# Last stage of a hybrid attention block on whole rows of 1024 columns, with the embedding vectors loaded earlier

## The chip, the cores and the metric

The kernel runs on one core of a Trainium2 chip. The metric is device time in microseconds (us), taken as the median of several runs. Before the change it is 712.65 us, the median of 3 runs (712.34 to 713.63). A separate execution was recorded by the hardware profiler; the lines shown in this document come from that one.

## The reference: what is computed

The reference is one decoder block over 528 positions (16 meta tokens and 512 inputs) of width 1024. After an input LayerNorm, ten projections are taken, two attention branches are computed and gated, the branches are merged and projected, and a residual LayerNorm gives the output. What matters for this change is the input LayerNorm, which is recomputed for the residual, and the end:

```python
h = layer_norm(h, emb_ln_g, emb_ln_b)
...
br_d = jnp.einsum('blw,wd->bld', y_d * jax.nn.silu(g_d), w_br_diff[i])
br_s = jnp.einsum('blw,wd->bld', y_s * jax.nn.silu(g_s), w_br_sb[i])
merged = jax.nn.sigmoid(m_d + b_gate[i, 0]) * br_d + jax.nn.sigmoid(m_s + b_gate[i, 1]) * br_s
y = jnp.einsum('bld,de->ble', merged, w_out[i])
h = layer_norm(DN_ALPHA * h + y, ln_g[i], ln_b[i])
...
return h[:, N_META:].astype(x.dtype)
```

## The kernel before

**Numbers and splitting.** Every product of float32 matrices is done as three matrix products of a high and a low part (`hh`, `hl`, `lh`). A weight arrives by DMA as a half tile `raw` (128 x 4 x 128), ScalarE (ACT) casts it to its high part `wh` (`hi`, line 183), and VectorE (DVE) subtracts to get the low part `wl` (`lo`, line 188). Both come from rings of six buffers, one ring for `wh` and one for `wl`; they are made four halves ahead of their use (`prep`, `state["ahead"]`).

**Stages.** First comes the input LayerNorm with its transposes. Then there are sixteen attention units (eight differential heads, eight pairs of stick-breaking heads), in which TensorE (PE) does the projections of the next unit (lines 494 to 496, 510, 690) between the scores (754), transposes (766) and values of this one. `stage_q` (line 604) makes a unit's queries; its second half, line 612, is a DVE operation `low` that reads a PSUM bank. Then come the merge gates of the first branch, four pairs of branch products ("BD", line 1065), the second set of merge gates (line 1099), four pairs "BS", and the last stage.

**What sets the order.** Each engine executes its own queue in order. For the attention units the order inside each queue is found by the framework's scheduler, which works from a model of time and from when the buffers come free; only the order in which work is written is given. From the merge gates on (`first`, line 1026) `keep_order` (line 1229) fixes the written order on PE, DVE, ACT, POOL (GpSimd) and SP, whose queue issues most DMAs.

**The last stage** (lines 1145 to 1229) makes y for 4 blocks `t` of 128 positions times 2 halves `c` of 512 columns. The loop runs over `c` outside and `t` inside. For each (c, t), 24 products of line 1190 fill one of three PSUM banks `pso`; the very last one, c=1 and t=3, is made as two banks of 256 columns. DVE then adds the residual (1198) and takes statistics (1201). With c=1 the row is complete: 1206 aggregates, POOL computes the reciprocal root `frs` (lines 296 and 297), and `shift` (1211) and `scale` (1215) apply the LayerNorm, in the order shift of half 0, scale of half 0, shift of half 1, scale of half 1. For t=3 a quarter row is scaled on ACT (1221) and POOL (1222) instead. Line 1227 stores two halves per block.

The residual `hr` is a half row of x, 128 x 512, loaded by line 1157 into a buffer of the `wh` or `wl` ring; lines 1161 and 1162 apply the input LayerNorm to it with the vectors `eg` and `eb`, of which line 1154 loads a half, spread over all partitions. `load_half(0)` and `load_half(1)` issue two such vectors and four half rows each. Between the blocks, `MEANWHILE` (line 1175) places on DVE the residuals and the splitting of the second half of `w_out` (`split_out`, lines 1126 and 1127, whose `fetch` issues the next load of `w_out` on SP). The vectors of the output LayerNorm, `lgb`, are loaded from ACT's queue (1196, 1197).

Of the kernel before, what the change touches and what calls it, by code (L numbers as in the profile page):

```python
# [45 lines left out]
def hybrid_block_kernel(ctx: ExitStack, tc: tile.TileContext, x, meta, emb_g, emb_b, w_in, b_gate,  # L46
# [128 lines left out]
    def hi(h):  # L175

        assert len(split) == h
        item = items[h]
# [4 lines left out]
        s.copy(wh, raw)  # L183
# [961 lines left out]
    def half(tag, name):  # L1145
        return wpool.tile([P, 4, P], F32, tag=tag, name=name, bufs=6).rearrange("p a b -> p (a b)")

    vec, hrs = {}, [[None, None] for t in range(NB)]

    def load_half(c):  # L1150
        tag = ("wh", "wl")[c]
        for name, src in (("eg", emb_g), ("eb", emb_b)):
            vec[name, c] = half({"eg": "wh", "eb": "wl"}[name], name)
            nc.sync.dma_start(vec[name, c], src[ts(c, 512)].partition_broadcast(P))
        for t in range(NB):
            hrs[t][c] = half(tag, "hr")
            nc.sync.dma_start(hrs[t][c], x[0, ts(t, P), ts(c, 512)])

    def residual(t, c):
        hr = hrs[t][c]  # L1160
        v.scalar_tensor_tensor(hr, hr, xmv[:, t, 0:1], vec["eg", c], op0=ALU.subtract, op1=ALU.mult)
        v.scalar_tensor_tensor(hr, hr, xrs[:, t:t + 1], vec["eb", c], op0=ALU.mult, op1=ALU.add)
# [12 lines left out]
    MEANWHILE = [[lambda: residual(0, 0)] + [lambda k=k: split_out(1, k) for k in range(3)],
                 [lambda: residual(1, 0)] + [lambda k=k: split_out(1, k) for k in range(3, 6)],
                 [lambda: residual(2, 0)] + [lambda k=k: split_out(1, k) for k in range(6, 8)] + [lambda: residual(0, 1)],
                 [lambda: residual(3, 0)] + [lambda t=t: residual(t, 1) for t in range(1, 3)],
                 [lambda: residual(3, 1)], [], [], []]
    for c in range(2):  # L1180
        for t in range(NB):
            st, final = sts[t], t == NB - 1
            for o, w in [(0, 256), (256, 256)] if final and c else [(0, 512)]:
                r, hr = ds(o, w), hrs[t][c]
# [24 lines left out]
            def shift(c, o, w):  # L1209
                a = hrs[t][c][:, ds(o, w)]  # L1210
                v.scalar_tensor_tensor(a, a, mv[:, 0:1], lgb[0][:, ds(512 * c + o, w)], op0=ALU.subtract, op1=ALU.mult)

            def scale(c, o, w):
                a = hrs[t][c][:, ds(o, w)]
                v.scalar_tensor_tensor(a, a, rs, lgb[1][:, ds(512 * c + o, w)], op0=ALU.mult, op1=ALU.add)  # L1215
# [43 lines left out]
```

## Time and profile before

| what | value |
|---|---|
| runs of the kernel before, us | 713.63, 712.65, 712.34 |
| the profiled execution, us | 712.22 |
| its span in the trace, us | 710.4 |
| PE busy, share of the span | 98% |
| DVE busy | 80% |
| ACT busy | 62% |
| POOL busy | 18% |

The profiled execution took 712.22 us, of which the trace's span covers 710.4. A row of a timeline has the start in us from the start of the span, the busy time in us, the engine, the source line, the operation, the tiles written and read, shapes, how often it came in a row, and in brackets the idle time before it with what ended it. "SPq" and "ACTq" are the queues of engines that issue DMAs. PE's operations are pipelined, so that a matmul of 512 columns shows 0.39 us, while the next one starts 0.23 us after it.

### The profile page before, as it was taken

To read this page: it belongs to the slowest core of one execution; us is meant where nothing else is said; L and a number is where in the kernel's file an instruction comes from. 1 tells how busy PE (TensorE), PEld (TensorE's weight loads), DVE (VectorE), ACT (ScalarE), POOL (GpSimd) and SP (SyncE) were. 2 spreads that over 40 slices of the span, in tenths; PEclk is the share of its full clock that TensorE was granted. 3 is DMA by queue.
4 is the path that set the end of the run, shared out by engine and by line. 5 is a ranking of instruction groups with operands and counts; after the bars stand their busy time and mean duration, and the time that the engine had idled before them with its cause. 6 is when DMAs were issued, how large, how long until landed. Compare 5 with 4: busy or idle time off the path is not lost.

```text
span 710.4 us, 13389 instructions
## 1 busy us (share of the span) xinstructions
PE 697.5 (98%) x4494; PEld 636.9 (90%) x4494; DVE 571.8 (80%) x1265; ACT 439.2 (62%) x1065; POOL 125.6 (18%) x143
## 2 busy tenths in 40 slices
PE   9999999999999999999999999999999999999994
PEld 8999999989999898988989998988889998999884
DVE  6888897878787777988878889976666788788897
ACT  5766676757667587776857777666455546455300
POOL 3214210212222111212123120000012102220002
PEclk9999999999999999999999999999999999999997
DMA  9368754879888876899897976646576748795902
GB/s 293 93 169 164 167 133 125 184 181 183 198 200 184 201 177 164 186 215 214 200 217 174 206 171 175 166 133 197 178 174 112 164 123 182 133 198 170 322 15 104
DMA packets 182182, 123.36 MB, mean 174 GB/s; under 512 B 9009, under 2 KB 165074, under 8 KB 182114
## 3 DMA queue, kind: packets, MB, share of 16 engines
q1 hardware_dynamic: 148130, 102.32, 50.1%
q0 software_dynamic: 33664, 19.14, 21.6%
q10 hardware_dynamic: 320, 1.06, 0.4%
q8 instruction: 35, 0.57, 0.3%
q14 instruction: 33, 0.27, 0.1%
HBM read 91.96 MB, written 9.44 MB: 143 GB/s over the span
## 4 chain that ended last, share of the span: by engine, by line
PE 86%; DVE 6%; DMA 3%; ACT 2%; issue 1%; POOL 1%; SPq 0%; ACTq 0%; DVEq 0%; POOLq 0%
PE q L690 16%; PE ps L496 12%; PE ps L494 12%; PE ps L495 12%; PE q L1065 10%; PE ps L510 7%; PE sc L754 6%; PE t L766 4%; DMA lgb<-in_ln_b_dram 1%; PE bank L385 1%; PE tv L723 1%; DVE hr L1215 1%; DMA xt<-in_x_dram 1%; PE av L922 1%; DMA raw<-in_w_out_dram 1%
## 5 line engine op out<-in xcount | busy, mean ns | idle before, releaser
L188 DVE TENSOR_TENSOR wl<-raw,wh 128x512 fp32r<-128x512 f32 x169 | 115.7, 691 | 43.7 <-ACT wh L183 42.2
L494 PE MATMUL ps<-hTh,wh 128*128 128x512 f32 x368 | 145.0, 394 | 0.0
L495 PE MATMUL ps<-hTl,wh 128*128 128x512 f32 x368 | 144.5, 393 | 0.0
L496 PE MATMUL ps<-hTh,wl 128*128 128x512 f32 x368 | 144.4, 392 | 0.0
L183 ACT CAST wh<-raw 128x512 fp32r<-128x512 f32 x169 | 104.4, 625 | 28.0 <-PE ps L495 15.3
L496 PEld LDWEIGHTS ps<-hTh,wl 128*128 128x128 f32 x368 | 69.2, 188 | 13.9
L495 PEld LDWEIGHTS ps<-hTl,wh 128*128 128x128 f32 x368 | 69.2, 188 | 13.1
L494 PEld LDWEIGHTS ps<-hTh,wh 128*128 128x128 f32 x368 | 69.2, 188 | 12.9
L146 POOL DMA_DIRECT2D rawk<-in_w_in_dram x44 | 60.8, 1642 | 96.9 <-DMA rawk<-in_w_in_dram 58.4
L754 PE MATMUL sc<-k,A 128*128 128x264 f32 (+3 forms) x320 | 65.9, 299 | 0.1
L1065 PE MATMUL q<-gh,wh 128*128 128x256 f32 x224 | 63.5, 283 | 0.2 <-ACT t L1074 0.2
L1065 PE MATMUL q<-gl,wh 128*128 128x256 f32 x224 | 63.4, 283 | 0.0
L1065 PE MATMUL q<-gh,wl 128*128 128x256 f32 x224 | 63.4, 283 | 0.0
L907 DVE TENSOR_TENSOR_SCAN e<-e,diag 128x528 f32<-128x528 f32 (+1 forms) x64 | 53.4, 848 | 7.5 <-ACT e L901 7.3
L754 PEld LDWEIGHTS sc<-k,A 128*128 128x128 f32 x320 | 50.3, 189 | 3.3 <-ACT e L901 0.3
L690 PE MATMUL q<-tS,wh 128*128 128x264 f32 x176 | 50.9, 290 | 0.9 <-DVE low L612 0.9
L690 PE MATMUL q<-tl,wh 128*128 128x264 f32 x176 | 50.2, 286 | 0.0
L690 PE MATMUL q<-tS,wl 128*128 128x264 f32 x176 | 50.2, 286 | 0.0
L510 PE MATMUL ps<-hTh,wh 128*128 128x264 f32 x160 | 46.4, 290 | 0.2 <-ACT k L632 0.2
L933 POOL DMA_DIRECT2D ys<-half x14 | 11.8, 840 | 195.9 <-ACT ys L932 119.2
L510 PE MATMUL ps<-hTh,wl 128*128 128x264 f32 x160 | 45.6, 286 | 0.0
L510 PE MATMUL ps<-hTl,wh 128*128 128x264 f32 x160 | 45.5, 285 | 0.0
(291 smaller groups left out, 1851.4 us busy)
## 6 DMA issues: line engine op xcount, KB each, us to landing
raw<-in_w_in_dram SPq DMA_DIRECT2D x141, 256.0 KB, 3.3
rawk<-in_w_in_dram POOLq DMA_DIRECT2D x44, 256.0 KB, 6.0
rawk<-in_w_in_dram SPq DMA_DIRECT2D x33, 256.0 KB, 3.9
k<-ks SPq DMA_DIRECT2D x60, 132.0 KB, 3.1
raw<-in_w_out_dram SPq DMA_DIRECT2D x16, 256.0 KB, 3.9
k<-ks SPq DMA_DIRECT2D x60, 66.0 KB, 2.8
A<-low SPq DMA_DIRECT2D x28, 128.0 KB, 2.8
raw<-in_w_br_diff_dram SPq DMA_DIRECT2D x12, 256.0 KB, 4.7
```

What stands on the lines that cost most here:

```text
L146: second[l] = [lambda raw=raw, x=x: g.dma_start(raw, x, accum_op=ALU.add) for x in more]
L183: s.copy(wh, raw)
L188: eng.tensor_tensor(wl, raw, wh.bitcast(F32), op=ALU.subtract)
L494: pe.matmul(ps, wh[:, k % 4, :], hTh[:, k, M:], start=(k == 0), stop=False)
L495: pe.matmul(ps, wh[:, k % 4, :], hTl[:, k, M:], start=False, stop=False)
L496: pe.matmul(ps, wl[:, k % 4, :], hTh[:, k, M:], start=False, stop=(k == KT - 1))
L510: pe.matmul(ps[:, :H2], a[:, k % 4, :], b[:, k, ts(c, H2)], start=(k == 0 and m == 0), stop=(k == KT - 1 and m == 2))
L690: pe.matmul(bank, a[:, k, :], b, start=start and k == 0 and j == 0, stop=k == 3 and j == 2, skip_group_check=not start)
L754: pe.matmul(ps[:, :n], q, K[:, m, k0:k0 + n], start=(m == 0), stop=(m == 1))
L766: pe.transpose(t[:, o:o + P], a[:, AOFF[i] + j * P:AOFF[i] + (j + 1) * P], ident)
L907: v.tensor_tensor_scan(rev, rev, diag[0][:, L - nk:][:, ::-1], 0.0, ALU.mult, ALU.max)
L1065: pe.matmul(bank, a[:, k, :], b[:, n, k, :], start=start and k == 0 and m == 0, stop=k == 3 and m == 2, skip_group_check=not start)
```

## The change

There are four edits.

- `wh` and `wl` of a weight half become two halves of one tile `w2` in one ring of six buffers.
- `eg` and `eb` are loaded whole, 1024 columns each, from SP, between the pairs "BD" and the second set of merge gates, into the ring "two" of `pair_of`.
- The last stage works on whole rows. A row of x is one load of 128 x 1024 into a buffer of `w2`; `residual(t)` is two DVE operations of 1024 columns. Row 0 is loaded after `split_out(0, 5)`, rows 1 to 3 behind the residual of the row before. `lgb` takes two buffers of `w2` and is loaded when t=2. In `MEANWHILE` the splitting stands ahead of the residual.
- `shift` is one operation of 1024 columns, and `scale` follows it directly, also 1024 columns wide; for t=3 it is two of 512 columns, each followed by its store. The quarter on ACT and POOL is gone. Blocks 0 to 2 are stored by one DMA each.

```diff
-        wh, wl = [wpool.tile([P, 4, P], F32R, tag=w, name=w, bufs=6) for w in ("wh", "wl")]
+        w2 = wpool.tile([P, 2, 4, P], F32R, tag="w2", name="w2", bufs=6)
+        wh, wl = w2[:, 0], w2[:, 1]
...
     ss = [pair_of("ss", n=S) for j in range(3)]
+    vec = {}
+    for name, src in (("eg", emb_g), ("eb", emb_b)):
+        vec[name] = pair_of(name, n=512).rearrange("p a b -> p (a b)")
+        nc.sync.dma_start(vec[name], src.partition_broadcast(P))
...
+    def load_rows(t):
+        hrs.append(whole("hr"))
+        nc.sync.dma_start(hrs[t], x[0, ts(t, P), :])
+
+    def residual(t):
+        hr = hrs[t]
+        v.scalar_tensor_tensor(hr, hr, xmv[:, t, 0:1], vec["eg"], op0=ALU.subtract, op1=ALU.mult)
+        v.scalar_tensor_tensor(hr, hr, xrs[:, t:t + 1], vec["eb"], op0=ALU.mult, op1=ALU.add)
...
-    load_half(0)
     for k in range(5, KT):
         split_out(0, k)
-    load_half(1)
+        if k == 5:
+            load_rows(0)
...
-    MEANWHILE = [[lambda: residual(0, 0)] + [lambda k=k: split_out(1, k) for k in range(3)],
...
+    MEANWHILE = [[lambda k=k: split_out(1, k) for k in range(3)] + [lambda: residual(0), lambda: load_rows(1)],
...
-                    if t == 0 and c == 0:
-                        nc.scalar.dma_start(lgb[0][:, :], ln_g[0].partition_broadcast(P))
-                        nc.scalar.dma_start(lgb[1][:, :], ln_b[0].partition_broadcast(P))
+                    if t == 2 and c == 0:
+                        for src in (ln_g, ln_b):
+                            lgb.append(whole("lgb"))
+                            nc.scalar.dma_start(lgb[-1], src[0].partition_broadcast(P))
...
-            shift(0, 0, 512)
-            if final:
-                a = hrs[t][1][:, 256:]
-                shift(1, 256, 256)
-                s.mul(a, a, rs)
-                g.tensor_tensor(a, a, lgb[1][:, 768:], op=ALU.add)
-            scale(0, 0, 512)
-            shift(1, 0, 256 if final else 512)
-            scale(1, 0, 256 if final else 512)
-            for h in range(2):
-                nc.sync.dma_start(out[0, ts(t, P), ts(h, 512)], hrs[t][h])
+            shift(0, D)
+            if not final:
+                scale(0, D)
+                nc.sync.dma_start(out[0, ts(t, P), :], hrs[t])
+                continue
+            scale(0, 512)
+            nc.sync.dma_start(out[0, ts(t, P), :512], hrs[t][:, :512])
+            scale(512, 512)
+            nc.sync.dma_start(out[0, ts(t, P), 512:], hrs[t][:, 512:])
```

The instructions move in three places. The first is DVE's queue at the end of the program, from the statistics of block t=3 on. Before:

```order
L1198 SCALAR_TENSOR_TENSOR hr<-hr,pso 128x256
L1201 BN_STATS fst<-hr 128x6
L1206 BN_AGGR fmv<-fst 128x2
L1211 SCALAR_TENSOR_TENSOR hr<-hr,fmv,lgb 128x512
L1211 SCALAR_TENSOR_TENSOR hr<-hr,fmv,lgb 128x256
L1215 SCALAR_TENSOR_TENSOR hr<-hr,frs,lgb 128x512
L1211 SCALAR_TENSOR_TENSOR hr<-hr,fmv,lgb 128x256
L1215 SCALAR_TENSOR_TENSOR hr<-hr,frs,lgb 128x256
```

The same place after the change, where the line numbers are one less:

```order
L1197 SCALAR_TENSOR_TENSOR hr<-hr,pso 128x256
L1200 BN_STATS fst<-hr 128x6
L1205 BN_AGGR fmv<-fst 128x2
L1210 SCALAR_TENSOR_TENSOR hr<-hr,fmv,lgb 128x1024
L1214 SCALAR_TENSOR_TENSOR hr<-hr,frs,lgb 128x512 x2
```

Five operations behind the aggregate have become three, and the shift of the whole row stands ahead of the first scaling, which needs POOL's `frs`.

The second place is SP's queue from the last loads of `w_out` to the stores. Before:

```order
L144 DMA raw<-in_w_out_dram 128x512 x11
L1154 DMA eg<-in_emb_ln_g_dram 128x512
L1154 DMA eb<-in_emb_ln_b_dram 128x512
L1157 DMA hr<-in_x_dram 128x512 x4
L144 DMA raw<-in_w_out_dram 128x512 x3
```

Behind these five rows stand a second group of `eg`, `eb` and four half rows, the last two loads of `w_out`, and eight stores. After the change there is in their place:

```order
L144 DMA raw<-in_w_out_dram 128x512 x12
L1157 DMA hr<-in_x_dram 128x1024
L144 DMA raw<-in_w_out_dram 128x512 x4
L1157 DMA hr<-in_x_dram 128x1024 x3
L1219 DMA out_dram<-hr 128x1024 x3
```

All sixteen loads of `w_out` now stand ahead of the rows 1 to 3, with row 0 between them.

The third place lies in an attention unit of the stick-breaking branch. There the scheduler has drawn up all queues anew, since the buffers of `wh` and `wl` now come free together. DVE's queue around the last `low` of `stage_q` (`e` and `apad` belong to the scores of a unit, `al` and `ax` to its transposes, `sg` to a gate), before:

```order
L188 TENSOR_TENSOR wl<-raw,wh 128x512
L907 SCALAR_TENSOR_TENSOR e_447<-e_447,diag 128x528
L772 TENSOR_TENSOR al_6114<-t_6108,ah_6113 128x512
L908 TENSOR_TENSOR apad_433<-e_446,e_447 128x527
L788 TENSOR_TENSOR ax<-t_6120,own_block 128x128
L612 SCALAR_TENSOR_TENSOR low<-ps,A_6137 128x512
L524 TENSOR_TENSOR sg<-ps,sg 128x512
L188 TENSOR_TENSOR wl<-rawk,wh 128x512
```

And after the change, where a low part is called `w_` with a number:

```order
L189 TENSOR_TENSOR w_6113<-raw,w_6113 128x512
L908 SCALAR_TENSOR_TENSOR e_443<-e_443,diag 128x528
L909 TENSOR_TENSOR apad_429<-e_442,e_443 128x527
L189 TENSOR_TENSOR w_6148<-rawk,w_6148 128x512
L773 TENSOR_TENSOR al_5970<-t_5964,ah_5969 128x512
L789 TENSOR_TENSOR ax<-t_5976,own_block 128x128
L613 SCALAR_TENSOR_TENSOR low<-ps,A_5993 128x512
L525 TENSOR_TENSOR sg<-ps,sg 128x512
```

Here the low part made from `rawk` has moved from behind the gate to ahead of `low`. Such moves run through all units of the attention stage on PE, DVE, ACT and SP; POOL's queue keeps its order, but for the operation of line 1222, which is gone.

More of the change, by code (lines that the diff above doesn't have):

```diff
@@ L1142, in hybrid_block_kernel, with whole @@
         run([pair("BS", p, G, MS[2 * p:2 * p + 2], lambda m, p=p: merged(2 * p + m))], steps)
[L1145 to L1162, printed above, removed]
+    def whole(name):
+        return wpool.tile([P, 2, 4, P], F32, tag="w2", name=name, bufs=6).rearrange("p a b c -> p (a b c)")
+    hrs = []
+    def load_rows(t):
[5 more added lines that the diff above has]
+        v.scalar_tensor_tensor(hr, hr, xrs[:, t:t + 1], vec["eb"], op0=ALU.mult, op1=ALU.add)
     for _, f in later:
@@ L1166, in hybrid_block_kernel @@
     later.clear()
-    load_half(0)
     for k in range(5, KT):
         split_out(0, k)
-    load_half(1)
+        if k == 5:
+            load_rows(0)
     WO.append([lp.tile([P, KT, 512], F32R, tag=f"g{x}", name=f"wo1{x}") for x in "hl"])
-    lgb = [pair_of("lgb", n=512) for j in range(2)]
-    lgb = [t.rearrange("p a b -> p (a b)") for t in lgb]
+    lgb = []
     sts = [lr.tile([P, 4, 6], F32, tag="fst", name="fst", bufs=4) for t in range(NB)]
-    MEANWHILE = [[lambda: residual(0, 0)] + [lambda k=k: split_out(1, k) for k in range(3)],
[L1176 to L1179, printed above, removed]
+    MEANWHILE = [[lambda k=k: split_out(1, k) for k in range(3)] + [lambda: residual(0), lambda: load_rows(1)],
+                 [lambda k=k: split_out(1, k) for k in range(3, 6)] + [lambda: residual(1), lambda: load_rows(2)],
+                 [lambda k=k: split_out(1, k) for k in range(6, 8)] + [lambda: residual(2), lambda: load_rows(3)],
+                 [lambda: residual(3)], [], [], [], []]
     for c in range(2):
@@ L1183, in hybrid_block_kernel @@
             for o, w in [(0, 256), (256, 256)] if final and c else [(0, 512)]:
[L1184 removed]
+                r, hr = ds(o, w), hrs[t][:, ts(c, 512)]
                 ps = pj.tile([P, 512], F32, tag="pj", name="pso")[:, :w]
@@ L1207, in hybrid_block_kernel, with shift, scale @@
             rstd_of(lr, mv[:, 1:2], rs, P)
[L1209 to L1215, printed above, removed]
-            shift(0, 0, 512)
-            if final:
-                a = hrs[t][1][:, 256:]
-                shift(1, 256, 256)
-                s.mul(a, a, rs)
-                g.tensor_tensor(a, a, lgb[1][:, 768:], op=ALU.add)
-            scale(0, 0, 512)
-            shift(1, 0, 256 if final else 512)
-            scale(1, 0, 256 if final else 512)
-            for h in range(2):
-                nc.sync.dma_start(out[0, ts(t, P), ts(h, 512)], hrs[t][h])
+            def shift(o, w, t=t, mv=mv):
+                a = hrs[t][:, ds(o, w)]
+                v.scalar_tensor_tensor(a, a, mv[:, 0:1], lgb[0][:, ds(o, w)], op0=ALU.subtract, op1=ALU.mult)
+            def scale(o, w, t=t, rs=rs):
+                a = hrs[t][:, ds(o, w)]
+                v.scalar_tensor_tensor(a, a, rs, lgb[1][:, ds(o, w)], op0=ALU.mult, op1=ALU.add)
+            shift(0, D)
[7 more added lines that the diff above has]
+            nc.sync.dma_start(out[0, ts(t, P), 512:], hrs[t][:, 512:])
     keep_order(state["ends"], ORDERED[:1])
```

## The prediction

> **What bounds the kernel now.** The page and the time by stretches come first, since they say where there is room at all.
>
> ```profile
> span 710.4 us, 13389 instructions
> 30.00:560.00 530.00, 528.70 (x3415) 482.71 (x3414) 424.99 (x983) 359.66 (x901) 98.71 (x98) 1.00 0.77 178
> 701.00:711.00 10.00, 0.00 (x0) 0.00 (x0) 6.06 (x12) 0.51 (x1) 1.78 (x3) 0.59 0.27 106
> ```
>
> The first pair of columns is PE with its instructions, the third DVE. From 30 to 560 us PE is busy for 528.70 of 530 us at full granted clock (1.00): all room there is 1.3 us. From 701 us on PE does nothing, and DVE works for 6 us. So the end must be read from the timeline of the last stage: PE's first and last row there, then the other engines.
>
> ```profile
> 656.42 0.40 PE L1190 MATMUL pso<-wo0h,mh 128*128 128x512 f32 x1
> 700.40 0.28 PE L1190 MATMUL pso<-wo1h,ml 128*128 128x256 f32 x1
> 701.95 0.41 DVE L1198 SCALAR_TENSOR_TENSOR hr<-hr,pso 128x256 f32<-128x256 f32 x1
> 702.40 0.43 DVE L1201 BATCH_NORM_STATS2 fst<-hr 128x6 f32<-128x256 f32 x1
> 702.74 0.40 DVE L1198 SCALAR_TENSOR_TENSOR hr<-hr,pso 128x256 f32<-128x256 f32 x1
> 703.18 0.43 DVE L1201 BATCH_NORM_STATS2 fst<-hr 128x6 f32<-128x256 f32 x1
> 703.64 0.26 DVE L1206 BATCH_NORM_AGGREGATE fmv<-fst 128x2 f32<-128x24 f32 x1
> 703.94 1.17 DVE L1211 SCALAR_TENSOR_TENSOR hr<-hr,fmv,lgb 128x512 f32<-128x512 f32 x2
> 705.16 0.75 DVE L1215 SCALAR_TENSOR_TENSOR hr<-hr,frs,lgb 128x512 f32<-128x512 f32 x1
> 705.83 0.97 DVE L1211 SCALAR_TENSOR_TENSOR hr<-hr,fmv,lgb 128x256 f32<-128x256 f32 x1
> 706.83 0.48 DVE L1215 SCALAR_TENSOR_TENSOR hr<-hr,frs,lgb 128x256 f32<-128x256 f32 x1
> 704.25 0.87 POOL L297 TENSOR_TENSOR frs<-lne,neghalf 128x1 f32<-128x1 f32 x1
> 690.56 17.15 SPq L1227 DMA_DIRECT2D out_dram<-hr  x8
> ```
>
> PE's last product ends at 700.40 + 0.28 = 700.7, but DVE takes up the second-to-last bank only at 701.95 and the last at 702.74: it is 2.0 us behind PE. Its last operation ends at 706.83 + 0.48 = 707.3; the last store is issued at once (690.56 + 17.15 = 707.7 ends the issue), and the span ends at 710.4, 3.1 us behind DVE. So DVE sets the end. The block before, with the same half c=1, shows why it is behind:
>
> ```profile
> 696.93 0.68 DVE L1198 SCALAR_TENSOR_TENSOR hr<-hr,pso 128x512 f32<-128x512 f32 x1
> 697.64 0.69 DVE L1201 BATCH_NORM_STATS2 fst<-hr 128x6 f32<-128x512 f32 x1
> 698.37 0.21 DVE L1206 BATCH_NORM_AGGREGATE fmv<-fst 128x2 f32<-128x12 f32 x1
> 698.62 0.78 DVE L1211 SCALAR_TENSOR_TENSOR hr<-hr,fmv,lgb 128x512 f32<-128x512 f32 x1
> 699.84 0.75 DVE L1215 SCALAR_TENSOR_TENSOR hr<-hr,frs,lgb 128x512 f32<-128x512 f32 x1 [0.44 <-POOL frs L297]
> 700.50 0.74 DVE L1211 SCALAR_TENSOR_TENSOR hr<-hr,fmv,lgb 128x512 f32<-128x512 f32 x1
> 701.28 0.75 DVE L1215 SCALAR_TENSOR_TENSOR hr<-hr,frs,lgb 128x512 f32<-128x512 f32 x1
> ```
>
> A block costs DVE 701.95 - 696.93 = 5.02 us, of which 0.44 is a wait for POOL. PE needs (700.7 - 656.4) / 8 = 5.5 us per block of 512 columns, so DVE gains only half a microsecond per block and carries its lag from the first half of the stage to the end.
>
> **The change part by part: shift and scale.** The width of 1024 stands in the trace once, on DVE, in another stage:
>
> ```profile
> 587.03 1.23 DVE L1047 TENSOR_TENSOR gl<-t,gh 128x1024 fp32r<-128x1024 f32 x1 [0.18 <-ACT gh L1046]
> ```
>
> From 256 to 512 columns L1215 goes from 0.48 to 0.75 us, 0.27 per 256 columns; two such steps more are 1.29 us for 1024. The row of 1.23 is a simpler operation and agrees. The bounds are 1.23 and twice 0.75 = 1.50; I take 1.29. An operation that does not depend on the one ahead starts 0.66 us after it at 512 columns (699.84 to 700.50), one that does 0.78 (700.50 to 701.28), so 0.09 before or 0.04 behind its end. [...]
>
> Blocks 0 to 2 of c=1 then cost 1.44 (696.93 to 698.37) + 0.25 + 1.33 + 1.21 = 4.23 us instead of 5.02. The wait for POOL is covered: `frs` ended 705.12 - 703.90 = 1.22 us behind the aggregate's end in the last block, and the shift of 1024 columns takes 1.29 of that. If the cover were gone, it would cost the 0.44 again.
>
> The last block: from the aggregate's start to the end of the last scaling stand 707.31 - 703.64 = 3.67 us before. After: 0.30 + 1.33 (shift) + 0.66 + 0.75 (two scalings) = 3.04. That is 0.63 less, and POOL and ACT, beside which a shift of 256 columns took 0.97 us, have left.
>
> **The lag.** If DVE waits for PE at the end, the last bank is taken up at about 700.8, not 702.74, and the tail starts at 700.8 + (703.64 - 702.74) = 701.7: 1.94 us earlier. PE's own time stays (same 24 products per bank). So the question is whether DVE catches up, which the first half of the stage decides:
>
> ```profile
> 659.43 1.89 DVE L1127 TENSOR_TENSOR wo0l<-raw,wo0h 128x512 fp32r<-128x512 f32 x3
> 663.03 0.75 DVE L1161 SCALAR_TENSOR_TENSOR hr<-hr,xmv,eg 128x512 f32<-128x512 f32 x1 [1.71 <-DMA hr<-in_x_dram]
> 660.15 3.19 SPq L144 DMA_DIRECT2D raw<-in_w_out_dram  x3
> hr<-in_x_dram SPq DMA_DIRECT2D x8, 256.0 KB, 5.9
> 658.86 10.32 DMA lgb<-in_ln_b_dram
> ```
>
> Row 0 is issued behind the load that SP issued at 660.15, so at about 660.6. With the median of 5.9 us it lands at 666.5. Ahead of it DVE splits three parts (659.43 to 661.3) and three more (1.9 us), until 663.2: the old wait of 1.7 us becomes one of about 3.3. From then on, with a residual at 1.33 + 1.21 = 2.54, a split at 1.89 / 3 = 0.63 and L1198 with L1201 at 1.4, the four blocks of c=0 (three splits in the second, two in the third) cost 3.94, 5.83, 5.20 and 3.94, in all 18.9, so DVE is at 685.4 when PE's fifth bank is ready (656.4 + 5 x 5.5 = 684). Three blocks of 4.23 end at 698.1. Bound by PE, the third block would start when its bank is ready, at 700.7 - 5.5 = 695.2, and end at 699.4; the two quarters need 0.79 ahead of the last bank. So DVE has about 0.5 us in hand at the end, and another 1.3 at the start: row 0 may land as late as 668.3. The Trainium skill ("DMA: Bandwidth & Descriptors", section "Anatomy of one DMA") puts a transfer at 2.0 us plus its bytes by 436 GB/s, by which the whole row lands 0.6 us later than a half and speaks against joining loads; by it the row lands at 663.8 (an estimate: 3.2 us), by the rows at 666.5, and the sum is the same by both.
>
> **Loads.** The vectors stand on SP ahead of the loads for the first pair "BS":
>
> ```profile
> 584.35 0.37 SPq L144 DMA_DIRECT2D raw<-in_w_br_sb_dram  x1
> 589.77 2.59 POOL L146 DMA_DIRECT2D rawa<-in_w_br_sb_dram  x2 [30.86 <-DMA rawa<-in_w_br_sb_dram]
> rawa<-in_w_br_sb_dram POOLq DMA_DIRECT2D x8, 256.0 KB, 5.9
> 604.03 0.62 ACT L183 CAST wh<-rawa 128x512 fp32r<-128x512 f32 x1
> out_dram<-hr SPq DMA_DIRECT2D x8, 256.0 KB, 2.0
> ```
>
> Two issues of about 0.4 us and 1 MB are added. Their buffers held `ydT`, whose last readers ran before the pairs "BD", so SP waits for nothing. Behind them queue the `raw` and `rawa` loads, for these POOL's adding DMAs, for those ACT's cast at 604.03. That chain ends at 589.77 + 2.59 + 5.9 = 598.3, 5.8 us ahead of the cast. A vector of this size took 10.32 us in the crowded last stage (the `lgb` row above), 4.4 more than a half row there; a delay of 4.4 is within the 5.8, so I take nothing. Without that cover a late cast would hold up PE by what exceeds it. The last two loads of `w_out` lose their place behind eight half rows, and DVE's waits for them go. The stores of block 3 come 0.7 us apart instead of 1.4; each takes 2.0 us, which bounds the cost by 1.3 us; the DMA engines are 0.27 busy there (701 to 711 us, above), so I take nothing.
>
> **The attention stage.** The queues are drawn up anew, as the third place above shows. What ACT's cast waited for, and PE from 30 us on (us in all, times, longest):
>
> ```profile
> L183 ACT CAST wh<-raw 128x512 fp32r<-128x512 f32 x169 | 104.4, 625 | 28.0 <-PE ps L495 15.3
> PE q L690 <- DVE low L612: 0.9, 2, 0.6
> PE ps L510 <- ACT k L632: 0.2, 1, 0.2
> PE q L1065 <- ACT t L1074: 0.2, 1, 0.2
> 440.15 0.39 PE L690 MATMUL q<-tS,wh 128*128 128x264 f32 x1 [0.63 <-DVE low L612]
> ```
>
> The ring `w2` makes the cast wait for the product behind L495, 5.5 / 24 = 0.23 us later; PE uses the tile four halves later, so I take nothing. For the new order the bound below is all idle time, 1.3 us of gain. Above, a wait like the one at 440.15 in each of 15 units would be 15 x 0.63 = 9.5 us. I take zero: the same scheduler with the same work, and in the old order two waits in all; it is nearest to that row.
>
> **Sum.** 1.94 + 0.63 = 2.57 us less, span 707.9. Against the profiled execution's 712.2 that is 709.6; this execution lay 0.4 under the median of 712.65, so for the median 710.1 us. About 0.2%, 1.4 us, can be told from no change.
>
> **The rivals.** (1) The new order costs PE 1.2 to 4 us in the attention stage, so that the gain is eaten: 711.3 to 714.1. For it speaks that a low part now stands ahead of the last `low`, 0.6 us on DVE, just where PE waited; against it that the other operations ahead of it are the same as before. Chance 0.2. (2) DVE does not catch up, since row 0 comes late: from 668.3 on each microsecond is lost. With the 10.3 us that `lgb` took, it lands at 670.9, the loss is 2.6, and the time 712.7. Against it: `lgb` shared its time with ten other transfers, row 0 with five. Chance 0.07. (3) Slower: PE waits at L690 for `low` once per unit. From 4.0 us more of such waits (2.6 + 1.4) the kernel is slower than before; that is eight units at 0.63 less the 0.9 there now, 714.2, and with all 15 it is 718.7. Against it: in the old order two units did. Chance 0.08. (4) The new order removes PE's waits: 0.9 to 1.3 more, 709. Chance 0.08.
>
> **How the numbers follow.** The forecast has 0.57: 709.2 to 711.2, from the 0.2 to 0.3 by which the wide operations may differ five times and the stores. Faster by over 0.2% (under 711.2) are the forecast, (4), and 0.04 of the edges of (1) and (2): 0.69. Within 0.2%: the rest of (1) but its upper end, and of (2): 0.21. Slower: (3) and 0.02 of (1): 0.10. The range reaches from 708.9, rival (4), to 712.7, which leaves out (3) and the upper part of (1).
>
> **What would show it.** Right: in the last block DVE's L1198 waits for PE in both quarters, no wait for `frs`, operations of 1.29 us, DVE's end near 704.7, PE's last product still near 700.4. Wrong: PE's last product later than 701.5 (the attention stage has paid), or DVE without waits for PE in blocks 1 to 3 of c=1, or a wait for `hr` of more than 5 us.

## The result, and the profile after

| | before | after |
|---|---|---|
| runs, median (lowest to highest), us | 712.36 (711.76 to 713.63), 10 runs | 710.65 (710.26 to 711.77), 10 runs |
| profiled execution, us | 712.22 | 710.71 |
| span, us | 710.4 | 708.9 |
| PE's first and last product of the last stage start at, us | 656.42, 700.40 | 657.05, 701.04 |
| DVE takes up the last bank at, us | 702.74 | 701.36 |
| aggregate of the last block starts at, us | 703.64 | 702.27 |
| last scaling ends at, us | 707.31 | 705.74 |

The ratio is 0.9979 (95% interval 0.997 to 0.9988): 1.7 us faster where 2.57 were forecast. The first rows of the timeline after show DVE in the first half of the last stage, with SP's issue of row 0:

```profile
657.05 0.40 PE L1188 MATMUL pso<-wo0h,mh 128*128 128x512 f32 x1
661.15 0.42 SPq L1157 DMA_DIRECT2D hr<-in_x_dram  x1
661.86 1.89 DVE L1132 TENSOR_TENSOR wo1l<-raw,wo1h 128x512 fp32r<-128x512 f32 x3
665.12 1.29 DVE L1161 SCALAR_TENSOR_TENSOR hr<-hr,xmv,eg 128x1024 f32<-128x1024 f32 x1 [1.37 <-DMA hr<-in_x_dram]
684.73 0.69 DVE L1197 SCALAR_TENSOR_TENSOR hr<-hr,pso 128x512 f32<-128x512 f32 x1 [0.29 <-PE pso L1188]
```

DVE waits 1.37 us for row 0, although it has already done three splits that stood behind that wait before. At 684.73 it is the other way round: DVE waits for PE's fifth bank. It has caught up before the half c=1 begins. The same timeline from the block t=2 of c=1 to the end:

```profile
695.61 0.69 DVE L1197 SCALAR_TENSOR_TENSOR hr<-hr,pso 128x512 f32<-128x512 f32 x1 [0.71 <-PE pso L1188]
697.30 1.31 DVE L1210 SCALAR_TENSOR_TENSOR hr<-hr,fmv,lgb 128x1024 f32<-128x1024 f32 x1
699.05 1.29 DVE L1214 SCALAR_TENSOR_TENSOR hr<-hr,frs,lgb 128x1024 f32<-128x1024 f32 x1 [0.44 <-POOL frs L298]
700.25 0.41 DVE L1197 SCALAR_TENSOR_TENSOR hr<-hr,pso 128x256 f32<-128x256 f32 x1
701.04 0.28 PE L1188 MATMUL pso<-wo1h,ml 128*128 128x256 f32 x1
701.36 0.42 DVE L1197 SCALAR_TENSOR_TENSOR hr<-hr,pso 128x256 f32<-128x256 f32 x1 [0.23 <-PE pso L1188]
702.27 0.26 DVE L1205 BATCH_NORM_AGGREGATE fmv<-fst 128x2 f32<-128x24 f32 x1
702.57 1.31 DVE L1210 SCALAR_TENSOR_TENSOR hr<-hr,fmv,lgb 128x1024 f32<-128x1024 f32 x1
704.32 1.42 DVE L1214 SCALAR_TENSOR_TENSOR hr<-hr,frs,lgb 128x512 f32<-128x512 f32 x2 [0.44 <-POOL frs L298]
```

Three things are to be seen. DVE takes up the last bank 0.32 us behind PE, still waits for `frs`, and PE itself is late. In numbers, the last bank is taken up 701.36 - 701.04 = 0.32 us after the start of PE's last product, where it was 702.74 - 700.40 = 2.34: the lag is 2.02 us shorter. The wait for `frs` is still there, 0.44 us, in spite of a shift of 1.31 us beside which POOL works; so the tail from the aggregate's start to the last scaling's end is 705.74 - 702.27 = 3.47 us, 0.20 less than the 3.67 before. And PE's own last product is 0.64 us later. With 0.07 more between DVE's end and the span's end, that makes -2.02 - 0.20 + 0.64 + 0.07 = -1.51 us, which is the difference of the two spans.

Two things needed an experiment: why the wait for POOL stayed, and what made DVE catch up and PE late. The profile alone cannot tell which of the four edits did which.

### The profile page after: what moved, and what is told of

Read it like the earlier page. It is cut to its first block, busy times and chain, and to the rows that moved or that the text cites. A ratio compares the mean times of both kernels' runs of the same rounds, so it can differ in the third digit from the quotient of the medians.

```text
span 708.9 us, 13322 instructions
## 1 busy us (share of the span) xinstructions
PE 697.0 (98%) x4494; PEld 636.0 (90%) x4494; DVE 569.3 (80%) x1249; ACT 438.3 (62%) x1064; POOL 126.8 (18%) x142
## 3 DMA queue, kind: packets, MB, share of 16 engines
q10 hardware_dynamic: 320, 1.06, 0.4%
## 4 chain that ended last, share of the span: by engine, by line
PE 90%; ACT 3%; issue 2%; DMA 2%; DVE 2%; POOL 1%; POOLq 0%; DVEq 0%; SPq 0%; ACTq 0%
PE q L691 15%; PE ps L497 11%; PE ps L496 11%; PE ps L495 11%; PE q L1066 11%; PE ps L511 7%; PE pso L1188 6%; PE sc L755 5%; PE t L767 3%; PE bank L386 1%; PE tv L724 1%; DMA k<-ks 1%; PE av L923 1%; PE av L924 1%; DMA xt<-in_x_dram 1%
## 5 line engine op out<-in xcount | busy, mean ns | idle before, releaser
L189 DVE TENSOR_TENSOR w<-raw,w 128x512 fp32r<-128x512 f32 x169 | 114.8, 686 | 41.4 <-ACT w L184 39.0
L495 PE MATMUL ps<-hTh,w 128*128 128x512 f32 x368 | 145.0, 394 | 0.0
L497 PE MATMUL ps<-hTh,w 128*128 128x512 f32 x368 | 144.6, 393 | 0.0
L496 PE MATMUL ps<-hTl,w 128*128 128x512 f32 x368 | 144.3, 392 | 0.0
L184 ACT CAST w<-raw 128x512 fp32r<-128x512 f32 x169 | 104.1, 626 | 19.2 <-PE ps L497 9.9
L497 PEld LDWEIGHTS ps<-hTh,w 128*128 128x128 f32 x368 | 69.2, 188 | 13.9
L1066 PE MATMUL q<-gh,w 128*128 128x256 f32 x448 | 81.4, 283 | 0.2 <-ACT t L1075 0.2
L496 PEld LDWEIGHTS ps<-hTl,w 128*128 128x128 f32 x368 | 69.2, 188 | 13.0
L495 PEld LDWEIGHTS ps<-hTh,w 128*128 128x128 f32 x368 | 69.2, 188 | 12.8
L691 PE MATMUL q<-tS,w 128*128 128x264 f32 x352 | 75.1, 290 | 0.0
L1066 PEld LDWEIGHTS q<-gh,w 128*128 128x128 f32 x448 | 70.1, 192 | 0.5 <-ACT t L1075 0.4
L755 PE MATMUL sc<-k,A 128*128 128x264 f32 (+3 forms) x320 | 66.8, 298 | 1.3 <-DMA k<-ks 0.9
L511 PE MATMUL ps<-hTh,w 128*128 128x264 f32 x320 | 64.4, 288 | 0.2 <-ACT k L633 0.2
L755 PEld LDWEIGHTS sc<-k,A 128*128 128x128 f32 x320 | 50.3, 188 | 4.5 <-ACT e L904 1.9
L511 PEld LDWEIGHTS ps<-hTh,w 128*128 128x128 f32 x320 | 51.4, 188 | 0.6 <-ACT k L633 0.4
```

The costliest lines, as they stand in the source:

```text
L189: eng.tensor_tensor(wl, raw, wh.bitcast(F32), op=ALU.subtract)
L495: pe.matmul(ps, wh[:, k % 4, :], hTh[:, k, M:], start=(k == 0), stop=False)
L496: pe.matmul(ps, wh[:, k % 4, :], hTl[:, k, M:], start=False, stop=False)
L497: pe.matmul(ps, wl[:, k % 4, :], hTh[:, k, M:], start=False, stop=(k == KT - 1))
L511: pe.matmul(ps[:, :H2], a[:, k % 4, :], b[:, k, ts(c, H2)], start=(k == 0 and m == 0), stop=(k == KT - 1 and m == 2))
L691: pe.matmul(bank, a[:, k, :], b, start=start and k == 0 and j == 0, stop=k == 3 and j == 2, skip_group_check=not start)
```

## Experiments

All times are medians in us, compared with runs of the kernel before on the same chip (its median lay between 712.23 and 712.44). A microsecond is 0.14%.

| kernel | us (lowest to highest, runs) | ratio to before, 95% interval |
|---|---|---|
| half_blocks | 710.79 (710.27 to 712.25, 8) | 0.9978, 0.9968 to 0.9988 |
| early_vec | 710.46 (709.91 to 711.70, 9) | 0.9973, 0.9958 to 0.9987 |
| vec_late | 712.16 (711.81 to 713.08, 12) | 1.0000, 0.9991 to 1.0008 |
| ring_only | 712.75 (711.84 to 713.11, 11) | 1.0000, 0.9992 to 1.0009 |
| split_shift | 710.72 (709.41 to 711.55, 11) | 0.9975, 0.9966 to 0.9984 |
| psum_shift | 710.24 (709.68 to 711.06, 6) | 0.9969, 0.9958 to 0.9980 |
| old_rings | 709.50 (709.10 to 709.70, 5) | 0.9958, 0.9944 to 0.9971 |
| old_rings_2, old_rings_3 | 710.17 (7 runs), 709.35 (5 runs) | 0.9968, 0.9955 to 0.9980; 0.9961, 0.9947 to 0.9974 |
| after_2, after_3 | 710.26 (5 runs), 710.72 (11 runs) | 0.9970, 0.9958 to 0.9982; 0.9979, 0.9970 to 0.9988 |
| before_2 | 712.40 (1 run) | |

**Are the wide blocks what lets DVE catch up?** The changed kernel, with blocks 0 to 2 as they were:

```diff
-            shift(0, D)
-            if not final:
-                scale(0, D)
+            if final:
+                shift(0, D)
+            else:
+                for o in (0, 512):
+                    shift(o, 512)
+                    scale(o, 512)
```

> The changed kernel with the blocks 0 to 2 of c=1 as in the kernel before (shift, scale, shift, scale of 512 columns); the last block as in the changed kernel. A block then costs DVE about 5.0 us instead of 4.6 with its waits for PE (0.29, 0.44 and 0.71 us in the changed kernel, 1.44 in all), against 5.44 us that PE takes for one. Theory, that the whole-row operations of these three blocks only shorten DVE's waits for PE: 0 to 0.2 us above the changed kernel, 0.23 us at the most through the last wait. Rival, that the wide blocks are what lets DVE catch up: 3 x 0.8 less 1.67 = 0.7 us or more above the changed kernel, and DVE does not wait for PE in the last block.

It took 710.79 us, the same as the changed kernel (710.65). The timeline of the last block, PE's last product first:

```profile
701.02 0.28 PE L1188 MATMUL pso<-wo1h,ml 128*128 128x256 f32 x1
700.61 0.41 DVE L1197 SCALAR_TENSOR_TENSOR hr<-hr,pso 128x256 f32<-128x256 f32 x1
701.40 0.40 DVE L1197 SCALAR_TENSOR_TENSOR hr<-hr,pso 128x256 f32<-128x256 f32 x1
```

DVE is 0.38 us behind PE's last product instead of 0.32, with blocks of 5.0 us. It no longer waits for PE in the last block, as the rival has it, but it is only 0.06 us further behind, and the 0.7 us or more that the rival forecast are not there. So the rival falls: whole rows in these three blocks only shorten DVE's waits for PE.

**Is it the early load of the vectors?** First the change without it. The two loads stand on SP directly ahead of row 0:

```diff
-    for name, src in (("eg", emb_g), ("eb", emb_b)):
+    for name in ("eg", "eb"):
         vec[name] = pair_of(name, n=512).rearrange("p a b -> p (a b)")
-        nc.sync.dma_start(vec[name], src.partition_broadcast(P))
...
         if k == 5:
+            for name, src in (("eg", emb_g), ("eb", emb_b)):
+                nc.sync.dma_start(vec[name], src.partition_broadcast(P))
             load_rows(0)
```

> The changed kernel with the two embedding vectors loaded late, on SP's queue directly ahead of row 0, all else the same; so it lacks the early load alone. Row 0 then stands behind two transfers of 512 KB: its wait, 1.37 us in the changed kernel, grows by 2.5 to 5 us. The waits for PE in the blocks of c=1 (0.29 + 0.44 + 0.71 + 0.23 = 1.67 us) take up that much. Theory, that the early load is what lets DVE catch up: the waits for PE in the last blocks are gone, and the time is 1 to 3 us above the changed kernel. Rival, that the late loads run beside each other and cost row 0 under 1.7 us: within 0.3 us of the changed kernel.

It took 712.16 us: 1.9 more than the changed kernel that ran beside it on the same chip (710.26), and the same as the kernel before. The timeline shows SP's issue of row 0, DVE's wait for it, and PE's and DVE's last bank:

```profile
662.36 0.38 SPq L1156 DMA_DIRECT2D hr<-in_x_dram  x1
669.16 1.28 DVE L1160 SCALAR_TENSOR_TENSOR hr<-hr,xmv,eg 128x1024 f32<-128x1024 f32 x1 [5.19 <-DMA hr<-in_x_dram]
701.24 0.28 PE L1189 MATMUL pso<-wo1h,ml 128*128 128x256 f32 x1
703.36 0.40 DVE L1198 SCALAR_TENSOR_TENSOR hr<-hr,pso 128x256 f32<-128x256 f32 x1
```

The wait for row 0 grew from 1.37 to 5.19 us, by 3.8. The later issue (662.36 instead of 661.15) is 1.2 of it; most of the rest is that the row came 669.16 - 662.36 = 6.80 us after its issue and not 3.97, so that most of the delay arises after SP has issued it. The waits for PE of the changed kernel held 1.67 of it, which leaves 2.1; DVE's lag at the last bank is 703.36 - 701.24 = 2.12 instead of 0.32, 1.8 more. The theory holds, and the whole gain is gone with this one edit.

Then the other way round, the kernel before with this part alone:

```diff
     ss = [pair_of("ss", n=S) for j in range(3)]
+    vec = {}
+    for name, src in (("eg", emb_g), ("eb", emb_b)):
+        vec[name] = pair_of(name, n=512).rearrange("p a b -> p (a b)")
+        nc.sync.dma_start(vec[name], src.partition_broadcast(P))
...
-        for name, src in (("eg", emb_g), ("eb", emb_b)):
-            vec[name, c] = half({"eg": "wh", "eb": "wl"}[name], name)
-            nc.sync.dma_start(vec[name, c], src[ts(c, 512)].partition_broadcast(P))
...
-    lgb = [pair_of("lgb", n=512) for j in range(2)]
-    lgb = [t.rearrange("p a b -> p (a b)") for t in lgb]
+    lgb = [[half(tag, "lgb") for n in range(2)] for tag in ("wh", "wl")]
...
```

> The kernel before with one part of the change: the embedding vectors are loaded whole between the pairs BD and the second merge gates; lgb therefore lies in four halves in the rings wh and wl. Order and width of all operations of DVE stay as before, rows are half rows, the tail keeps its quarter on ACT and POOL. In the kernel before DVE waits in the first half of the stage 1.71 us for row 0 and 0.41 + 1.06 us for the last parts of w_out, and takes up the last bank 2.0 us after PE. Theory, that the early load alone lets DVE catch up: the three waits shrink by 1.5 to 3 us in all, DVE is at most 0.6 us behind PE at the last bank, and the time is 1.2 to 1.9 us under the kernel before. Rival, that the whole rows and the new order of splits and residuals are needed: under 0.6 us, the wait for row 0 still over 1 us.

It took 710.46 us, 1.92 under the kernel before: as much as the whole change. In its timeline:

```profile
661.03 0.74 DVE L1162 SCALAR_TENSOR_TENSOR hr<-hr,xmv,eg 128x512 f32<-128x512 f32 x1
667.40 1.90 DVE L1131 TENSOR_TENSOR wo1l<-raw,wo1h 128x512 fp32r<-128x512 f32 x3 [0.28 <-ACT wo1h L1130]
700.23 0.28 PE L1190 MATMUL pso<-wo1h,ml 128*128 128x256 f32 x1
700.63 0.40 DVE L1199 SCALAR_TENSOR_TENSOR hr<-hr,pso 128x256 f32<-128x256 f32 x1
```

Row 0 is there when DVE comes to it (661.03, where before it came at 663.03 after 1.71 us of waiting). The kernel before waited 1.71 + 0.41 + 1.06 = 3.18 us for row 0 and for the last parts of `w_out`; here 0.28 are left. DVE is 0.40 behind PE's last product. So DVE's lag in the kernel before was no matter of its own work: four vector loads stood on SP's queue ahead of what it needed. One thing beside them moved in this run, since `lgb` had to lie elsewhere; its second vector is issued in ACT's queue 6.3 us later than before (658.86):

```profile
665.12 1.59 ACTq L1198 DMA_DIRECT2D lgb<-in_ln_b_dram  x2
```

So this run alone doesn't separate the vectors' loads from that transfer. In "vec_late" `lgb` is late as well (issued from 671.73 on) and the gain is gone all the same. The early load is therefore shown to be needed; that it suffices is shown only together with the later `lgb`.

**What holds up POOL's root?** The root is `frs` of line 298, one number per partition. In the kernel before, the same operation at the start of the program (`xrs`) and in block t=2 of the last stage:

```profile
5.94 0.55 POOL L297 TENSOR_TENSOR xrs<-lne,neghalf 128x1 f32<-128x1 f32 x1
698.93 0.87 POOL L297 TENSOR_TENSOR frs<-lne,neghalf 128x1 f32<-128x1 f32 x1
```

and after the change, in the blocks t=0, with the addition `lne` ahead of it, and t=3:

```profile
686.47 1.29 POOL L297 TENSOR_TENSOR lne<-fmv,epsr 128x1 f32<-128x1 f32 x1 [41.70 <-DVE fmv L1205]
687.84 0.57 POOL L298 TENSOR_TENSOR frs<-lne,neghalf 128x1 f32<-128x1 f32 x1
702.61 0.19 POOL L297 TENSOR_TENSOR lne<-fmv,epsr 128x1 f32<-128x1 f32 x1 [3.60 <-DVE fmv L1205]
702.88 1.40 POOL L298 TENSOR_TENSOR frs<-lne,neghalf 128x1 f32<-128x1 f32 x1
```

An operation on one number takes 0.55 us alone, 0.87 beside a shift of 512 columns and 1.40 beside one of 1024. It ends at 704.28, 0.40 after the shift's end (702.57 + 1.31 = 703.88). In block t=0 the addition is the one that is held, for 1.29 us instead of 0.19, to just past the shift's end. In the other blocks the addition starts as close behind the shift's start (0.04 to 0.05 us) and is not held; the rows don't show why. Two experiments follow. The first halves the shift of the last block:

```diff
-            shift(0, D)
+            for o in (0, 512) if final else ():
+                shift(o, 512)
             if not final:
+                shift(0, D)
                 scale(0, D)
```

> The changed kernel with the shift of the last block as two operations of 512 columns, all else the same. In the changed kernel POOL's root (128x1) takes 1.40 us beside a shift of 1024 columns, ends 0.41 to 0.44 us behind the shift's end, and DVE waits 0.44 us for it. Theory, that POOL is held while this operation of DVE runs: in the last block the root ends 0.4 us behind the first half's end (near 703.7 us by the changed kernel's clock instead of 704.28), the wait for it is gone, and from the aggregate's start to the last scaling's end it takes 3.1 us instead of 3.47; 0.3 to 0.4 us less in all. Rival, that the root takes a fixed 1.4 us in this stage: it ends as late as now, the wait stays at 0.4 us, the time is the same.

The last block in its timeline, DVE and POOL:

```profile
702.97 0.26 DVE L1205 BATCH_NORM_AGGREGATE fmv<-fst 128x2 f32<-128x24 f32 x1
703.27 1.44 DVE L1210 SCALAR_TENSOR_TENSOR hr<-hr,fmv,lgb 128x512 f32<-128x512 f32 x2
703.58 0.87 POOL L298 TENSOR_TENSOR frs<-lne,neghalf 128x1 f32<-128x1 f32 x1
704.63 1.40 DVE L1214 SCALAR_TENSOR_TENSOR hr<-hr,frs,lgb 128x512 f32<-128x512 f32 x2
```

The root is back at 0.87, ends at 704.45 beside the second shift, and the wait is gone; the tail is 704.63 + 1.40 - 702.97 = 3.06 us instead of 3.47. A fixed time of POOL is ruled out. The median, 710.72, doesn't show the 0.41, since PE came 0.70 us later in this profile (657.75) and the runs spread over 2 us. The second experiment keeps the wide shift and changes where its second input lies; it reads one column of a PSUM bank over and over, so the kernel leaves out the multiplication by the norm's weight:

```diff
...
-                v.scalar_tensor_tensor(a, a, mv[:, 0:1], lgb[0][:, ds(o, w)], op0=ALU.subtract, op1=ALU.mult)
+                v.scalar_tensor_tensor(a, a, mv[:, 0:1], ps[:, 0:1].broadcast_to([P, w]), op0=ALU.subtract, op1=ALU.mult)
```

> The changed kernel with another second input of the shift: instead of the vector of 1024 columns in SBUF it reads one column of the PSUM bank pso, repeated 1024 times; so the multiplication by the norm's weight is left out. The shift keeps its width, its place and its operation. POOL's root took 0.55 us at the start of the program, 0.87 beside a shift of 512 columns, 1.40 beside one of 1024. Theory, that POOL is held because DVE's operation reads two inputs in SBUF: the root takes about 0.55 us, ends near 0.85 us behind the aggregate's end, beside the shift, and DVE does not wait for it; the last block takes 3.03 us instead of 3.47 from the aggregate's start, 0.4 us less in all. Rival, that POOL is held beside any DVE operation of that length: the root takes 1.4 us as now, and the wait of 0.44 us stays.

The last block in its timeline:

```profile
702.45 1.28 DVE L1210 SCALAR_TENSOR_TENSOR hr<-hr,fmv,pso 128x1024 f32<-128x1024 f32 x1
702.76 0.55 POOL L298 TENSOR_TENSOR frs<-lne,neghalf 128x1 f32<-128x1 f32 x1
703.84 1.42 DVE L1214 SCALAR_TENSOR_TENSOR hr<-hr,frs,lgb 128x512 f32<-128x512 f32 x2
```

The shift is as long as before, 1.28 us, and the root beside it takes 0.55, as it does alone. So it is not the length of DVE's operation but its second input, a vector in SBUF, that holds POOL. (The median, 710.24, equals the 710.26 of "after_2", which ran beside it; the tail is 703.84 + 1.42 - 702.15 = 3.11 us, but PE's last product came at 700.91, against 700.61 in the profile of "after_2".) The edit changes two things together, the memory of that input and its shape, one column repeated; no run here repeats a column in SBUF, so the runs alone do not tell the two apart. The Trainium skill ("SBUF — State Buffer", section "Who interferes with whom") names the memory: a DVE instruction with two inputs in SBUF contends with a GpSimd instruction that reads SBUF, and the contention for the ports that they share is an exclusive lock. The root's rows agree: 0.55, 0.87 and 1.40 us beside nothing, 512 and 1024 columns; the additions of 0.19 us beside the same shifts do not. The prediction did not use this rule.

**What does the new order of the attention stage cost?** The kernel before with the ring `w2` alone; its last stage takes halves from the tiles of `w2`:

```diff
-        wh, wl = [wpool.tile([P, 4, P], F32R, tag=w, name=w, bufs=6) for w in ("wh", "wl")]
+        w2 = wpool.tile([P, 2, 4, P], F32R, tag="w2", name="w2", bufs=6)
+        wh, wl = w2[:, 0], w2[:, 1]
...
-            hrs[t][c] = half(tag, "hr")
+            if c == 0:
+                hrs[t] = halves("hr")
```

> The kernel before with one of the four edits, the common ring w2; the last stage keeps its halves, which are taken from the tiles of w2, and all queues of the attention stage are the same as in the changed kernel. In the changed kernel's profile PE starts the last stage 0.64 us later (657.05 against 656.42 us). Theory, that the new order of the attention stage costs this: PE's first product of the last stage stands again near 657.05 us, its operations in the attention stage 0.6 to 0.7 us behind those of the kernel before from about 500 us on, and the time is 0.5 to 0.8 us above the kernel before. Rival, that executions scatter by as much: the start stands near 656.4 us, the time within 0.2 us of the kernel before.

It took 712.75 us, 0.3 over the kernel before, with an interval of -0.6 to +0.6 us. PE's first product of the last stage starts at 656.72, between the two forecasts. Neither theory is confirmed by this run. PE's waits as a list, of the changed kernel, and the row of the longest one:

```profile
PE sc L755 <- DMA k<-ks: 0.9, 1, 0.9
PE sc L755 <- ACT e L904: 0.3, 1, 0.3
```

```profile
341.40 0.48 PE L755 MATMUL sc<-k,A 128*128 128x264 f32 x2 [0.93 <-DMA k<-ks]
```

The two waits for `low` (0.9 us, near 314 and at 440.15) are gone from the list, and there is one for a DMA of keys, `k<-ks`, instead. SP's queue ahead of it, before:

```profile
334.71 1.12 SPq L644 DMA_DIRECT2D k<-ks  x2
335.92 0.55 SPq L614 DMA_DIRECT2D A<-A  x1
336.56 1.28 SPq L643 DMA_DIRECT2D k<-ks  x2
```

and after:

```profile
335.41 0.48 SPq L645 DMA_DIRECT2D k<-ks  x1
336.00 1.29 SPq L644 DMA_DIRECT2D k<-ks  x2
337.60 0.48 SPq L645 DMA_DIRECT2D k<-ks  x1
```

On SP the transfers of the keys stand in another order, and the last one is issued a few tenths later. PE's queue has changed at the same place, before:

```profile
340.01 0.41 PE L754 MATMUL sc<-k,A 128*128 128x264 f32 x2
340.25 0.28 PE L690 MATMUL q<-hTh,wh 128*128 128x264 f32 x1
...
341.00 0.48 PE L754 MATMUL sc<-k,A 128*128 128x264 f32 x2
```

In the kernel before, four products for `q` stand between the two pairs of scores, so that the second pair comes at 341.00 and the list shows no wait for it. In the changed kernel the second pair stands directly behind the first (340.07) and waits for its keys until 341.40. How long it waits depends on when they land, which differs from execution to execution. The repeats show it:

> The changed kernel again, for a second profile and more times beside the next kernel. So far the four profiles in the new order of the attention stage start the last stage at 656.72, 657.02, 657.05 and 657.75 us, each with a wait of PE of 0.5 to 1.6 us at L755 near 341 us; the two profiles in the old order start it at 655.94 and 656.42 without that wait. Theory, that the new order costs 0.5 to 1 us there: the wait at 341 us is there again, the start lies at 656.7 us or later. Rival, that all six are scatter: no wait there, or a start below 656.4.

> The changed kernel without the ring w2 again, beside the changed kernel itself. Theory, that its old order of the attention stage gains 0.6 us and the covered wait for POOL's root 0.41: no wait of PE near 341 us, the start of the last stage below 656.5 us, and 0.8 to 1.5 us less than the changed kernel in the same call. Rival, that only the covered wait counts and the rest was scatter: a start near 657 us in one of the two orders as in the other, and 0.4 us less.

> The kernel before again, for a second profile. The start of the last stage has been 656.42, 655.94 and 656.97 us in three profiles with the old order of the attention stage, 656.63 to 657.75 us (mean 657.05) in seven with the new. Theory, that it scatters by about 0.5 us in both orders: a start anywhere from 655.9 to 657.2. Rival, that the old order is a fixed 656.4 and the 656.97 an exception: 656.3 to 656.5. The last bank is taken up about 2 us after PE's last product, whatever the start, if DVE follows PE; less, if DVE's time is set by the loads.

> The changed kernel a third time, beside the kernel without the ring w2. By the theory the stall of PE near 340 us is there in most executions (0.4 to 1.6 us) and the start of the last stage lies between 656.6 and 657.8 us; 1.4 to 2.1 us under the kernel before.

Waits at L755, for keys or for ACT's `e`, are in all eight profiles with the ring `w2`, between 0.6 and 1.9 us in all (mean 1.16); the six profiles with separate rings have 0.9 us for `low` every time. The start of the last stage is 656.63 to 657.75 us (mean 657.02) with the ring and 655.94 to 656.97 (mean 656.42) without it. Both forecasts of "after_2" miss in part: the wait is there, but only 0.3 us at that place, and the start, 656.63, lies under the 656.7. In "old_rings_2" the start was 656.97, over the forecast 656.5, and the two kernels that ran side by side differed by 0.1 us only. In "before_2" the start is 656.65, within the theory's forecast and outside the rival's 656.3 to 656.5; the last bank is taken up 702.92 - 700.62 = 2.30 us behind PE, as in the first profile (2.34). "after_3" came as forecast, with a start of 656.83, 0.8 us of waits for keys, and 1.5 us under the kernel before. So the new order costs 0.6 us on average over these profiles, and one execution scatters by as much in either order. The waits named so far explain 0.3 of it, and less when the waits of PE for `al` at the transposes are counted too (0.2 to 0.3 us in four of the six profiles with separate rings and in three of the eight with `w2`): then 0.15 is left. What makes up the rest stays open.

**A kernel that takes the gain without the two costs.** The changed kernel with separate rings as before, rows in halves, and shift, shift, scale, scale of 512 columns:

```diff
-        w2 = wpool.tile([P, 2, 4, P], F32R, tag="w2", name="w2", bufs=6)
-        wh, wl = w2[:, 0], w2[:, 1]
+        wh, wl = [wpool.tile([P, 4, P], F32R, tag=w, name=w, bufs=6) for w in ("wh", "wl")]
...
-            shift(0, D)
...
+            shift(0)
+            shift(1)
+            for n in range(2):
+                scale(n)
+                nc.sync.dma_start(out[0, ts(t, P), ts(n, 512)], hrs[t][n])
```

> The changed kernel without the ring w2: wh and wl have rings of their own as before, so all queues of the attention stage are those of the kernel before; the last stage keeps the new order of loads, residuals and splits, with rows in two halves of 512 columns, and each block of c=1 is shift, shift, scale, scale of 512 columns with a store behind each scale. If the new order of the attention stage costs 0.64 us and the wider shift holds up POOL's root: PE's first product of the last stage stands near 656.4 us, POOL's root ends about 0.43 us behind the first shift and beside the second, DVE does not wait for it, the last block takes 0.30 + 0.66 + 0.66 + 0.66 + 0.75 = 3.03 us from the aggregate's start to the last scaling's end instead of 3.47, and the time is 0.64 + 0.44 = 1.1 us under the changed kernel, 2.8 us under the kernel before. Rival, that neither is so: 0.0 to 0.4 us from the changed kernel, the start near 657 us or the wait for the root still there. Beside that, DVE's residuals cost 1.4 us more in all (0.35 per row), which the waits for PE in the blocks of c=1 (1.7 us in all) still hold; if they do not, the last block of DVE does not wait for PE and up to 1 us of the gain is lost.

> The changed kernel without the ring w2, a third time, beside the changed kernel. The first comparison gave 1.1 us less than the changed kernel (of another call), the second 0.1 us less in one call. Theory: 0.41 us from the tail (POOL's root covered) and, on average, 0.4 us from the order of the attention stage, where the five profiles in the old order have one stall of PE of 0.86 us near 439 us, the seven in the new one of 0.47 us near 485 us and in six of them another of 0.4 to 1.6 us near 340 us: 0.4 to 1.2 us under the changed kernel of this call. Rival, that neither reaches the end: within 0.2 us of the changed kernel.

The end of its first timeline:

```profile
655.94 0.40 PE L1191 MATMUL pso<-wo0h,mh 128*128 128x512 f32 x1
699.91 0.28 PE L1191 MATMUL pso<-wo1h,ml 128*128 128x256 f32 x1
701.14 0.26 DVE L1209 BATCH_NORM_AGGREGATE fmv<-fst 128x2 f32<-128x24 f32 x1
701.44 1.44 DVE L1214 SCALAR_TENSOR_TENSOR hr<-hr,fmv,lgb 128x512 f32<-128x512 f32 x2
702.80 1.40 DVE L1218 SCALAR_TENSOR_TENSOR hr<-hr,frs,lgb 128x512 f32<-128x512 f32 x2
```

No wait for the root, a tail of 704.20 - 701.14 = 3.06 us. Its three medians are 709.50, 710.17 and 709.35, over all 17 runs 709.53; the changed kernel's three are 710.65, 710.26 and 710.72, over all 26 runs 710.58. That is 1.05 us less, near the 1.1 that was expected of the first run. The single comparisons give 1.15 (not run side by side), 0.1 and 1.37, so the second came out below its forecast of 0.8 to 1.5 and the third above its forecast of 0.4 to 1.2; the size is known only roughly. It is 2.9 us under the kernel before (712.38 over 82 runs).

## Why the prediction was right in sign and 0.9 us too large

**The lag (1.94 forecast, 2.02 measured): the size was right, the reason only in part.** DVE waits for PE in the blocks of c=1 (684.73, 695.61) and at the last quarter, as was forecast, though not at the first quarter (700.25). But the steps on the way were off. The wait for row 0 was forecast at 3.3 us and was 1.37, since the row landed 665.12 - 661.15 = 3.97 us after its issue and not 5.9; the estimate by the Trainium skill ("DMA: Bandwidth & Descriptors", section "Anatomy of one DMA"), 3.2 us, was nearer, though that section fits transfers issued by GpSimd and SP issued this one. Here two errors offset each other by luck: the prediction let the row land 1.9 us too late, and it set the latest landing that does no harm 1.5 us too late (rival (2) below). With the 5.9 the row would have landed at 667.05, just past the 666.8 that the rows allow. The blocks of c=1 cost 700.25 - 695.61 = 4.64 us, the 4.23 and the wait for `frs`. And the prediction let these shorter blocks work together with the first half; the runs show that they add nothing ("half_blocks") and that the early load does it ("vec_late", and "early_vec" with the later `lgb`). The prediction set the cost of the vector loads at their new place to nothing. For their old place it named only DVE's waits for the last two loads of `w_out`, without a price, and did not ask whether the early load alone would let DVE catch up.

**The tail (0.63 forecast, 0.20 measured): the step that failed is "The wait for POOL is covered".** The prediction set POOL's 1.22 us against a shift of 1.29. But the 1.22 was itself measured beside a shift of 512 columns, and it is not a time of POOL: it is the shift's length plus 0.4. A longer shift makes it longer by the same amount, so no shift in one piece can cover it. The price that the prediction named for this case, 0.44 us, is the one that was paid; "split_shift" and "psum_shift" each take it away.

**The attention stage (0 forecast, +0.64 in the profile, 0.6 on average).** The bounds held it, from -1.3 to +9.5. "Two waits in all" went, as rival (4) has it, but another came in their place, for a DMA, at a line that the prediction did not look at. Rival (1) named the right term at two to seven times its size; rival (3), one wait for `low` per unit, did not happen at all: that wait vanished.

**Loads and stores.** The vectors ahead of the pairs "BS" cost nothing there, as forecast. In the stretch from 560 to 655 us PE's busy time, the figure behind the 95.00, is the same before and after:

```profile
560.00:655.00 95.00, 94.81 (x662) 88.95 (x662) 77.03 (x148) 52.17 (x99) 15.66 (x14) 1.00 0.70 158
```

```profile
560.00:655.00 95.00, 94.80 (x662) 88.94 (x661) 76.94 (x147) 52.50 (x99) 15.66 (x14) 1.00 0.73 169
```

The last stores cost 0.07 us. The operation of 1024 columns took 1.28 to 1.31 us, 1.29 forecast. Of two independent scalings of 512 columns the rows show 1.42 us together, so the second starts before the first has ended, as in the rows of before.

**Rival (2)** was right as a mechanism and did not happen in the changed kernel; "vec_late" is that case. Its limit of 668.3 us for row 0 was too late: with 1.67 us of waits to spare behind a row at 665.1, the limit is 666.8. The blocks of c=1 carry waits for `frs` (0.73, 0.45 and 0.44 us) that the prediction had taken as covered.

In sum, 1.94 + 0.63 - 0 became 2.02 + 0.20 - 0.64 - 0.07 = 1.51 us in the profiles, 1.71 in the medians. The forecast of 710.1 us lay 0.55 under the median, inside its range; that it missed by less than the 0.86 by which the gain fell short is chance, since the kernel before came out 0.29 lower over ten runs (712.36) than over the three that were known (712.65).

## What to carry to other kernels

When an engine lags at the end, look for the transfer that it waited for half a stage earlier, and for what stands ahead of it on its queue: moving the loads of two vectors to an earlier place of that queue went with all of the gain, and making the operations of the blocks wider added nothing. A duration that was measured beside another operation is not a constant: before a wait is called covered, ask whether the cover is what makes it long. And a change of a buffer ring can redraw the order of a whole program; the cost is then small, scattered, and at a place that the change does not touch.

## What the runs showed of the hardware

- POOL's root on 128 x 1 elements, started beside a DVE operation with two tensor inputs in SBUF, ends about 0.4 us after that operation, whatever its length (0.87 us beside 512 columns, 1.40 beside 1024), and takes its own 0.55 us when DVE's second input is a repeated column in PSUM. It slips in between two such operations of DVE: in "split_shift" the second shift was not delayed by more than 0.04 us (1.44 for the pair, 1.40 for the pair of scalings).
- Executions of one and the same program start the last stage up to 1.0 us apart (655.94, 656.34 and 656.97 us in three profiles of the kernel with separate rings). A term of 0.4 us that is plain in every profile did not show in the medians of 6 and 11 runs ("psum_shift", "split_shift").
